# RWKV-7 chunk recurrence on Trainium2: the whole 64-block inverse ahead of the recurrence instead of a three-step solve inside it

## The chip, the cores and the metric

The kernel runs on one core of one Trainium2 chip. A core has a matrix engine (TensorE, PE in the profile, with PEld for its weight loads), a vector engine (VectorE, DVE), an activation engine (ScalarE, ACT), GpSimd (POOL), and a sync engine (SyncE, SP), whose queue here issues all DMA transfers. Each engine works off its own instructions in the order in which they were written, and waits where an operand is not there yet. The metric is device time in microseconds for one launch; lower is better.

## What the reference computes

One step of a decoder trunk of two layers, for 256 tokens of a prompt and 8 single tokens with saved states. In each layer a normalised input is projected; half of the columns go through RetNet retention (8 heads), half through RWKV-7 time mixing (16 heads of 64, worked on as 8 pairs); then come an output projection and a SwiGLU feed-forward network. The part that the change touches is the RWKV-7 scan over the prompt:

```
def step(s, inp):
    r_t, w_t, k_t, v_t, kk_t, a_t = inp
    sa = jnp.einsum('bhvk,bhk->bhv', s, -kk_t)
    s = (s * w_t[:, :, None, :] + sa[..., None] * (kk_t * a_t)[:, :, None, :]
         + v_t[..., None] * k_t[:, :, None, :])
    return s, jnp.einsum('bhvk,bhk->bhv', s, r_t)
```

Each step's `sa` depends on all earlier steps. Done in chunks of 64 tokens, that dependence inside a chunk is a unit lower triangular system (1 + L) Z = r, with L a 64x64 matrix for each head and chunk, and between chunks the state S is handed on.

## The kernel before

**The stream.** All weights (two layers, 6624 blocks of 128x128) are one stream. `Stream.load` fetches 8 blocks at a time (512 KB) into three `w_raw` buffers, on the sync queue; `Stream.make` splits four blocks at a time into a high part `w_hi` (ScalarE, L96) and a low part `w_lo` (VectorE, L99), three buffers of each, two groups of four ahead of the matmuls. Each block then multiplies the activations with three matmuls, in `proj` (L285 to L287) or in `contract` (L306 to L308). 

**The mixer between the blocks.** Every mixer step is a Python generator. After each block, `tick` lets those generators go on whose time has come; a generator's `yield n` means that n blocks are written before its next instructions. So the order of every engine's instructions is fixed when the program is written, and the yields are the only distance between an operand's producer and its reader on another engine. `need` and `take` tick without writing a block: if a slot of a pool is not free (`CAP`), all that is due is written out with no stream block between.

**A pair of RWKV heads.** `g_pair` prepares a pair: the triangular matrices `LA` and `KA` of its four chunks, and three transposed operands `TM` (three of eight slots that are shared with the tiles of the residual `h`). It may begin its later part only when the pair two before it has ended. `g_solve` (GpSimd) inverts the 16x16 diagonal blocks. `g_levels` merges pairs of them into inverses of 32x32 blocks, for four chunks at once: with the mask product m of L (L541, L526, GpSimd), Pm = m X (`pw<-X,Lm`, then a ScalarE copy, L549), and XT = XT - Pm XT (L552, L553). `X` and its transpose `XT` are then block diagonal with blocks of 32.

`g_seq` is the recurrence over the four chunks of a pair. For each chunk it writes: the product with `KA` and with the state S into `py` (L569, L571); from it `rT`, in two parts by VectorE and ScalarE (L574, L575); then the solve in three steps, `Z1` = X r (L587, copied by ScalarE at L590), `r1` = r - m1 Z1 (L594, subtracted by VectorE at L597) and Z = X r1 (L601, copied at L604); then the new state S (L607, L613) and the output (L617, L619). `m1` is the mask product for the second level, 32 to 64. Levels of one pair and the recurrence of another may overlap, but levels follow levels and recurrences follow recurrences (`spawn` with a kind).

**The layer.** `layer` writes the input projections of 8 pairs and 8 retention heads in the order of `ORDER`, then the output projection in three passes over 16 output blocks (`W_OUT`), during whose first pass `load_h` fetches the eight `h` tiles (each needs a `TM` slot), then the feed-forward network. Decode work for the single tokens (`g_rwkv_decode`: loads `dS`, products `dT`, reductions `dec_sa` and `dec_o`; `g_ret_state`: `rS`, `qkb`, `ryd`) runs beside it.

Of the kernel before, what the change touches and what calls it, by code (L numbers as in the profile page):

```python
# [11 lines left out]
F32 = mybir.dt.float32  # L12
F32R = mybir.dt.float32r
AF = mybir.ActivationFunctionType
ALU = mybir.AluOpType
# [4 lines left out]
P = 128  # L20
# [10 lines left out]
NC = SEQ // CW  # L31
# [13 lines left out]
TA, RR, LV, UB, U2 = 4, 2, 2, 6, 4  # L45
# [22 lines left out]
def bc(ap, axis, n):  # L68
    u = ap.unsqueeze(axis)
    s = list(u.shape)  # L70
    s[axis] = n
    return u.to_broadcast(s)
# [43 lines left out]


class Kern:
    """The main flow emits the weight stream: each 128x128 block is split into two float32r parts and multiplies the
    split activations in three passes. Every mixer step is a generator that yields the number of stream blocks to let  # L120
    pass before its next instructions, so that they reach the in-order engines when their operands are there."""

    def __init__(self, ctx, tc, a, o):
        self.tc, self.nc, self.a, self.o, self.ctx = tc, tc.nc, a, o, ctx
# [406 lines left out]
    def g_levels(self, t_solve, sv, LA):  # L531
        nc, rp = self.nc, self.rp
        yield from self.wait(t_solve)
        Xc = sv["X"]
        X = rp.tile([P, NC, P], F32, name="X", tag="lv", bufs=LV)
        XT = rp.tile([P, NC, P], F32, name="XT", tag="XT", bufs=2)

        def mm(lhsT, rhs):
            return lambda out, c: nc.tensor.matmul(out, lhsT=lhsT[:, c], rhs=rhs[:, c], start=True, stop=True)

        m = self.masked(LA, 0, "lv", LV)  # L541
        for q, t in enumerate((X, XT)):
            eng = nc.gpsimd if q else nc.vector
            eng.tensor_tensor(out=t.rearrange("p c (b k) -> p c b k", k=SB), in0=bc(Xc[:, q], 2, P // SB),
                              in1=bc(self.m_b8, 1, NC), op=ALU.mult)
        yield 8
        ps = yield from self.g_four(mm(m, X))
        Pm = rp.tile([P, NC, P], F32, name="Pm", tag="lv", bufs=LV)
        nc.scalar.activation(out=Pm, in_=ps, func=AF.Copy)  # L549
        self.pput()  # L550
        yield 5
        ps = yield from self.g_four(mm(Pm, XT))  # L552
        nc.vector.tensor_tensor(out=XT, in0=XT, in1=ps, op=ALU.subtract)  # L553
        self.pput()
        yield 4
        sv["XT"] = XT

    def g_seq(self, l, p, sv, AR, cf, LA, KA, TM, bv, Y):
        nc, rp, un = self.nc, self.rp, self.un
        XT = sv["XT"]  # L560
        m1 = self.masked(LA, 1, "m1", 1)
        o = rp.tile([P, 2, P], F32, name="o", tag="o", bufs=2)
        S = None
        lo, hi = slice(0, 64), slice(64, 128)
        for c in range(NC):
# [7 lines left out]
            rT = self.rT[:, c % 2]  # L573
# [8 lines left out]
                nc.scalar.activation(out=sc, in_=S, func=AF.Copy, scale=ct)  # L582
            pS = yield from self.pget()
            nc.tensor.matmul(pS[:, 0:P], lhsT=kT, rhs=vT, start=True, stop=False)
            yield 3
            pz = yield from self.pget()
            nc.tensor.matmul(pz[:, 0:P], lhsT=XT[:, c], rhs=rT, start=True, stop=True)  # L587
            yield 1
            Z1 = un.tile([P, P], F32, name="Z1", tag="u", bufs=UB)
            nc.scalar.activation(out=Z1, in_=pz[:, 0:P], func=AF.Copy)  # L590
            self.pput()
            yield 3
            pl = yield from self.pget()
            nc.tensor.matmul(pl[:, 0:P], lhsT=m1[:, c], rhs=Z1, start=True, stop=True)  # L594
            yield 1
            r1 = un.tile([P, P], F32, name="r1", tag="u", bufs=UB)
            nc.vector.tensor_tensor(out=r1, in0=rT, in1=pl[:, 0:P], op=ALU.subtract)  # L597
            self.pput()
            yield 3
            pz = yield from self.pget()  # L600
            nc.tensor.matmul(pz[:, 0:P], lhsT=XT[:, c], rhs=r1, start=True, stop=True)  # L601
            yield 1
            Z = un.tile([P, P], F32, name="Z", tag="Z", bufs=2)
            nc.scalar.activation(out=Z, in_=pz[:, 0:P], func=AF.Copy)  # L604
            self.pput()
            yield 3
            nc.tensor.matmul(pS[:, 0:P], lhsT=bT, rhs=Z, start=False, stop=True)  # L607
            yield 1
            Sn = un.tile([P, P], F32, name="S", tag="S", bufs=2)
# [2 lines left out]
            else:  # L612
# [6 lines left out]
            nc.vector.tensor_tensor(out=o[64 * (c % 2):64 * (c % 2) + 64, c // 2], in0=po[hi, 0:P], in1=oc[hi],  # L619
                                    op=ALU.add)  # L620
            self.pput()
            yield 2
        for hh in range(2):
            s = slice(64 * hh, 64 * hh + 64)
            nc.sync.dma_start(out=self.o["srp"][l, 2 * p + hh], in_=S[s, s])
# [808 lines left out]
```

## Time and profile before

| | us |
|---|---|
| three runs: median | 2919.91 |
| lowest, highest | 2918.66, 2921.32 |
| the profiled execution: its span, first to last instruction | 2925.0 |
| PE busy | 2799.1 (96%) |
| DVE busy | 2009.9 (69%) |
| ACT busy | 1416.1 (48%) |
| POOL busy | 806.9 (28%) |

The profile gives the span of its own execution and no other time of it. Busy time is the time in which at least one instruction of an engine is drawn; matmuls are pipelined, so their drawn ends overlap the next one's start. Every float32 matmul of the mixer is recorded as two, so that 64 calls (16 pairs x 4 chunks over two layers) are 128 records; a stream matmul is one record. An idle time in a row is that of the engine directly before the instruction, with the instruction that ended it.

### The profile page before, as it was taken

The page shows a single profiled execution, that of the slowest core. Times are in us where ns is not written, and L with a number is a line of the kernel's source. Part 1 is how long each engine was busy: PE and PEld are TensorE (multiplying, and loading weights), DVE is VectorE, ACT ScalarE, POOL GpSimd, SP SyncE. Part 2 cuts the span into 40 slices and gives each one's busy share as a digit, 9 for nine tenths or more (in the row PEclk, how much of TensorE's full clock was granted, in tenths as well). Part 3 has the DMA queues.
Part 4 walks back from the last instruction along what each step waited for, and adds up shares of the span by engine and source line. Part 5 has one row for each costly group of instructions (what it writes and reads, how often), then busy time and mean ns, then how long its engine had stood idle before and what let it go on. Part 6 is the DMA issues. An engine that isn't in the chain of part 4 may idle for free. (4 is left out here: it accounts for less than half of the span.)

```text
span 2925.0 us, 59208 instructions
## 1 busy us (share of the span) xinstructions
PE 2799.1 (96%) x22298; PEld 2755.2 (94%) x22298; DVE 2009.9 (69%) x3964; ACT 1416.1 (48%) x2823; POOL 806.9 (28%) x1316
## 2 busy tenths in 40 slices
PE   7998999999999999999999999999999999999998
PEld 7998999899999999999998888888999999999998
DVE  6677777887856656556766777778877565565665
ACT  5544455445444444444545445544544444444444
POOL 4545555434400000000234556554243000000002
PEclk9999999999999999999999999999999999999999
DMA  4454555565655555555654445556656555555554
GB/s 161 142 155 148 157 153 173 189 221 191 203 182 179 180 179 180 180 180 181 211 158 137 150 146 156 160 163 212 203 193 195 181 180 181 180 181 179 181 180 148
DMA packets 230832, 512.50 MB, mean 175 GB/s; under 512 B 57488, under 2 KB 105872, under 8 KB 230544
## 3 DMA queue, kind: packets, MB, share of 16 engines
q1 hardware_dynamic: 230544, 508.70, 54.6%
q8 instruction: 175, 2.87, 0.4%
q14 instruction: 113, 0.93, 0.1%
HBM read 485.24 MB, written 23.38 MB: 174 GB/s over the span
## 5 line engine op out<-in xcount | busy, mean ns | idle before, releaser
L99 DVE TENSOR_TENSOR w_lo<-w_raw,w_hi 128x512 fp32r<-128x512 f32 x1652 | 1240.4, 753 | 849.3 <-ACT w_hi L96 835.8
L96 ACT ACTIVATE w_hi<-w_raw 128x512 fp32r<-128x512 f32 x1656 | 1042.8, 631 | 1131.5 <-PE st L286 631.1
L285 PE MATMUL st<-blk,w_hi 128*128 128x264 f32 (+1 forms) x4704 | 1438.6, 306 | 11.9 <-ACT w_hi L96 7.4
L287 PE MATMUL st<-blk,w_lo 128*128 128x264 f32 (+1 forms) x4704 | 1353.0, 288 | 15.5 <-DVE w_lo L99 14.7
L286 PE MATMUL st<-blk,w_hi 128*128 128x264 f32 (+1 forms) x4704 | 1351.4, 287 | 1.0 <-DVE blk L1094 1.0
L287 PEld LDWEIGHTS st<-blk,w_lo 128*128 128x128 f32 x4704 | 895.0, 190 | 22.8 <-DVE w_lo L99 21.3
L285 PEld LDWEIGHTS st<-blk,w_hi 128*128 128x128 f32 x4704 | 896.2, 191 | 17.1 <-ACT w_hi L96 11.0
L286 PEld LDWEIGHTS st<-blk,w_hi 128*128 128x128 f32 x4704 | 898.0, 191 | 3.9 <-DVE blk L1094 2.0
L306 PE MATMUL st<-blk,w_hi 128*128 128x264 f32 x1920 | 551.0, 287 | 5.8 <-DVE h L1244 4.5
L307 PE MATMUL st<-blk,w_hi 128*128 128x264 f32 x1920 | 548.6, 286 | 0.0
L308 PE MATMUL st<-blk,w_lo 128*128 128x264 f32 x1920 | 546.7, 285 | 0.0
L1035 POOL TENSOR_TENSOR acc<-acc,sq 128x264 f32<-128x264 f32 x73 | 62.7, 860 | 1374.7 <-ACT sq L1032 1374.3
L306 PEld LDWEIGHTS st<-blk,w_hi 128*128 128x128 f32 x1920 | 361.0, 188 | 8.8 <-issue 4.0
L308 PEld LDWEIGHTS st<-blk,w_lo 128*128 128x128 f32 x1920 | 362.5, 189 | 0.1
L307 PEld LDWEIGHTS st<-blk,w_hi 128*128 128x128 f32 x1920 | 361.4, 188 | 0.1
L684 POOL TENSOR_TENSOR sv_t<-sv_m,sv_x 32x15 f32<-32x15 f32 (+7 forms) x240 | 90.0, 375 | 27.1 <-DMA sv_m<-scr_l 13.7
L1244 DVE TENSOR_TENSOR h<-h,st 128x264 f32<-128x264 f32 x224 | 94.1, 420 | 2.9 <-PE st L308 2.8
L686 POOL TENSOR_TENSOR sv_x<-sv_x,sv_t 32x15 f32<-32x15 f32 (+7 forms) x240 | 85.2, 355 | 18.8
L575 ACT ACTIVATE c_rT<-pw 64x64 f32<-64x64 f32 x64 | 13.8, 215 | 113.3 <-DVE c_rT L574 113.1
L323 ACT ACTIVATE mix_d<-mix_p,c_vec 128x256 f32<-128x256 f32 x54 | 27.5, 508 | 71.8 <-DVE mix_p L319 44.6
L899 POOL TENSOR_TENSOR qkb<-rS,qkb 128x512 f32<-128x512 f32 x32 | 44.5, 1391 | 58.9 <-DVE rS L896 58.9
L816 POOL TENSOR_TENSOR uS<-uS,dec_v 128x512 f32<-128x512 f32 x16 | 23.7, 1480 | 113.0 <-DMA uS<-in_s_rwkv 113.0
(251 smaller groups left out, 2636.5 us busy)
## 6 DMA issues: line engine op xcount, KB each, us to landing
w_raw<-in_ws SPq DMA_DIRECT2D x828, 512.0 KB
qkb<-scr_qk SPq DMA_DIRECT2D x64, 256.0 KB
rS<-in_s_ret SPq DMA_DIRECT2D x32, 256.0 KB
out_sts<-rS SPq DMA_DIRECT2D x32, 256.0 KB
h<-in_x SPq DMA_DIRECT2D x16, 264.0 KB
dS<-in_s_rwkv SPq DMA_DIRECT2D x16, 256.0 KB
uS<-in_s_rwkv SPq DMA_DIRECT2D x16, 256.0 KB
out_srs<-uS SPq DMA_DIRECT2D x16, 256.0 KB
```

Source lines behind the costliest of these rows:

```text
L96: nc.scalar.activation(out=h, in_=w, func=AF.Copy)
L99: eng.tensor_tensor(out=l, in0=w, in1=h.bitcast(F32), op=ALU.subtract)
L285: nc.tensor.matmul(ps, lhsT=hi, rhs=self.x[k][:, 0, 0:n], start=k == 0, stop=False)
L286: nc.tensor.matmul(ps, lhsT=hi, rhs=self.x[k][:, 1, 0:n], start=False, stop=False)
L287: nc.tensor.matmul(ps, lhsT=lo, rhs=self.x[k][:, 0, 0:n], start=False, stop=k == KB - 1)
L306: nc.tensor.matmul(ps, lhsT=hi, rhs=t[:, 0, 0:T], start=k == 0, stop=False)
L307: nc.tensor.matmul(ps, lhsT=hi, rhs=t[:, 1, 0:T], start=False, stop=False)
L308: nc.tensor.matmul(ps, lhsT=lo, rhs=t[:, 0, 0:T], start=False, stop=k == n - 1)
L684: nc.gpsimd.tensor_tensor(out=t, in0=bc(M[:, j, j + 1:SB], 2, j + 1), in1=bc(X0[:, j, 0:j + 1], 1, m), op=ALU.mult)
L686: nc.gpsimd.tensor_tensor(out=X0[:, j + 1:SB, 0:j + 1], in0=X0[:, j + 1:SB, 0:j + 1], in1=t, op=ALU.subtract)
L1035: nc.gpsimd.tensor_tensor(out=self.acc, in0=self.acc, in1=sq, op=ALU.add)
L1244: self.nc.vector.tensor_tensor(out=h, in0=h, in1=ps, op=ALU.add)
```

## The change

The loop over levels in `g_levels` now runs twice. The first pass is as before and ends with a transpose on VectorE, which works on blocks of 32x32: since `XT` is block diagonal in 32x32 blocks at that point, this gives the new `X`. The second pass uses the mask product `m1`, now made in the first pass, and leaves in `XT` the transposed inverse of the whole 64x64 block. `g_seq` then needs one matmul, Z = X r. The yields around it become 5, 1, 5 in place of 3, 1, 3, 1, 3, 1, 3, and the last one of a chunk 4 in place of 2. A comment of the class is replaced by blank lines. Code below the solve stands 8 lines further up than before. Its core:

```
@@ g_levels
-        ps = yield from self.g_four(mm(m, X))
-        Pm = rp.tile([P, NC, P], F32, name="Pm", tag="lv", bufs=LV)
-        nc.scalar.activation(out=Pm, in_=ps, func=AF.Copy)
-        self.pput()
-        yield 5
-        ps = yield from self.g_four(mm(Pm, XT))
-        nc.vector.tensor_tensor(out=XT, in0=XT, in1=ps, op=ALU.subtract)
-        self.pput()
+        for lev in range(2):
+            ps = yield from self.g_four(mm(m, X))
+            Pm = rp.tile([P, NC, P], F32, name="Pm", tag="lv", bufs=LV)
+            nc.scalar.activation(out=Pm, in_=ps, func=AF.Copy)
+            self.pput()
+            if lev == 0:
+                m = self.masked(LA, 1, "m1", 1)
+            yield 5
+            ps = yield from self.g_four(mm(Pm, XT))
+            nc.vector.tensor_tensor(out=XT, in0=XT, in1=ps, op=ALU.subtract)
+            self.pput()
+            if lev == 0:
+                X = rp.tile([P, NC, P], F32, name="X", tag="lv", bufs=LV)
+                nc.vector.transpose(X.rearrange("p c q -> p (c q)"), XT.rearrange("p c q -> p (c q)"))
+                yield 7
         yield 4
@@ g_seq
-        m1 = self.masked(LA, 1, "m1", 1)
...
             nc.tensor.matmul(pS[:, 0:P], lhsT=kT, rhs=vT, start=True, stop=False)
-            yield 3
+            yield 5
             pz = yield from self.pget()
             nc.tensor.matmul(pz[:, 0:P], lhsT=XT[:, c], rhs=rT, start=True, stop=True)
-            yield 1
-            Z1 = un.tile([P, P], F32, name="Z1", tag="u", bufs=UB)
-            nc.scalar.activation(out=Z1, in_=pz[:, 0:P], func=AF.Copy)
-            self.pput()
-            yield 3
-            pl = yield from self.pget()
-            nc.tensor.matmul(pl[:, 0:P], lhsT=m1[:, c], rhs=Z1, start=True, stop=True)
-            yield 1
-            r1 = un.tile([P, P], F32, name="r1", tag="u", bufs=UB)
-            nc.vector.tensor_tensor(out=r1, in0=rT, in1=pl[:, 0:P], op=ALU.subtract)
-            self.pput()
-            yield 3
-            pz = yield from self.pget()
-            nc.tensor.matmul(pz[:, 0:P], lhsT=XT[:, c], rhs=r1, start=True, stop=True)
             yield 1
             Z = un.tile([P, P], F32, name="Z", tag="Z", bufs=2)
             nc.scalar.activation(out=Z, in_=pz[:, 0:P], func=AF.Copy)
             self.pput()
-            yield 3
+            yield 5
...
-            yield 2
+            yield 4
```

How the order of instructions changes is shown at three places. The first is ScalarE in the recurrence of the first pair, one chunk, from its `rT` to its `Z`. Before:

```order
L575 ACTIVATE c_rT<-pw 64x64
L577 ACTIVATE oc<-pw 64x128
L582 ACTIVATE Sc<-S,cf 128x128
L96 ACTIVATE w_hi<-w_raw 128x512
L590 ACTIVATE Z_1926<-pw 128x128
L96 ACTIVATE w_hi<-w_raw 128x512 x2
L604 ACTIVATE Z<-pw 128x128
```

With the change:

```order
L581 ACTIVATE c_rT<-pw 64x64
L583 ACTIVATE oc<-pw 64x128
L588 ACTIVATE Sc<-S,cf 128x128
L96 ACTIVATE w_hi<-w_raw 128x512
L596 ACTIVATE Z<-pw 128x128
```

The copy `Z1` (L590, named Z_1926) and two splits of weights between it and `Z` are gone from the chunk.

The second place is VectorE at the levels of the first pair, with the stream's `w_lo` around it. Before:

```order
L553 TENSOR_TENSOR XT<-XT,pw 128x512
L99 TENSOR_TENSOR w_lo<-w_raw,w_hi 128x512
L319 TENSOR_TENSOR mix_p<-st,c_R 128x272
L574 TENSOR_SCALAR c_rT<-pw 64x64
L99 TENSOR_TENSOR w_lo<-w_raw,w_hi 128x512
```

With the change:

```order
L556 TENSOR_TENSOR XT<-XT,pw 128x512
L560 STREAM_TRANSPOSE X<-XT 128x512
L99 TENSOR_TENSOR w_lo<-w_raw,w_hi 128x512
L319 TENSOR_TENSOR mix_p<-st,c_R 128x272
L99 TENSOR_TENSOR w_lo<-w_raw,w_hi 128x512
```

The transpose follows directly on the subtraction, and the first `c_rT` of the recurrence is no longer here: the recurrence begins 24 blocks later, after a second subtraction into `XT`.

The third place is early in the output projection of the first layer, block 968 of 3312. The last stream matmul before and the first one behind are shown with what TensorE now has between them (TM, KA, AR, LA and XT are operands of pair 7's recurrence, `on` belongs to a retention head):

```order
L308 MATMUL st<-blk,w_lo 128x264
L575 MATMUL pw<-TM_6749,KA 128x128
L577 MATMUL pw<-S,AR 128x128
L590 MATMUL pw<-TM_6749,TM_6748 128x128
L593 MATMUL pw<-c_rT,XT 128x128
L599 MATMUL pw<-Z,TM_6747 128x128
L356 MATMUL pw<-c_ident,on 128x128 x2
L609 MATMUL pw<-Z,LA 128x128
L306 MATMUL st<-blk,w_hi 128x264
```

And VectorE between two `w_lo` at the same place, with the change:

```order
L611 TENSOR_TENSOR o<-pw,oc 64x128
L1236 TENSOR_TENSOR h<-h,st 128x264
L760 TENSOR_TENSOR dT<-dS,dec_wr 128x512
L762 TENSOR_REDUCE dec_o<-dT 128x8
L580 TENSOR_SCALAR c_rT<-pw 64x64
L1236 TENSOR_TENSOR h<-h,st 128x264
L710 TENSOR_SCALAR on<-ryt,bmv,brs 128x128 x2
L762 TENSOR_REDUCE dec_sa<-dT 128x8
L888 SCALAR_TENSOR_TENSOR rS<-rS,qkb_8113 128x512
L605 SCALAR_TENSOR_TENSOR S<-pw,cf,Sc 128x128
...
L99 TENSOR_TENSOR w_lo<-w_raw,w_hi 128x512
```

Left out are `dT`, o, `ry` and `dec_o`, one each. Before, the same position of both engines holds stream work with one or two mixer instructions between groups:

```order
L99 TENSOR_TENSOR w_lo<-w_raw,w_hi 128x512
L1244 TENSOR_TENSOR h<-h,st 128x264
L718 TENSOR_SCALAR on<-dec_o,bmv,brs 128x64
L650 SCALAR_TENSOR_TENSOR y<-y,c_vec,pw 128x256
L99 TENSOR_TENSOR w_lo<-w_raw,w_hi 128x512
```

What moved: the last chunk of pair 7, which before stood among the input projections up to block 928, now stands at block 968 in one piece, with what else was due. The second layer has the same place.

## Rows read from the trace of the kernel before

**Rows 1.** The page's first part: busy time (share of the span) x instructions.

```profile
PE 2799.1 (96%) x22298; PEld 2755.2 (94%) x22298; DVE 2009.9 (69%) x3964; ACT 1416.1 (48%) x2823; POOL 806.9 (28%) x1316
```

**Rows 2.** Stretches: length, busy PE, PEld, DVE, ACT, POOL (instructions), clock, DMA share, GB/s.

```profile
73.00:585.00 512.00, 473.42 (x3706) 459.82 (x3704) 381.18 (x875) 250.29 (x597) 271.50 (x504) 0.98 0.52 160
585.00:690.00 105.00, 102.30 (x826) 100.78 (x825) 85.73 (x167) 55.92 (x109) 38.98 (x56) 1.00 0.64 208
1530.00:2050.00 520.00, 478.18 (x3707) 461.33 (x3707) 394.62 (x909) 254.94 (x605) 279.71 (x504) 0.98 0.52 160
```

**Rows 3.** Waits of PE by line: total us, times, longest us.

```profile
PE pw L601 <- DVE r L597: 22.1, 20, 2.4
PE pw L587 <- ACT c_rT L575: 19.0, 17, 3.0
...
PE pw L571 <- DVE S L613: 5.0, 5, 3.0
...
PE pw L594 <- ACT Z L590: 2.0, 5, 0.9
PE pw L569 <- DVE S L613: 1.8, 2, 1.5
```

**Rows 4.** Timeline of PE around 331 us: start, length, instruction, [idle before, what ended it].

```profile
331.25 0.46 PE L601 MATMUL pw<-r,XT 128*128 128x128 f32 x2 [2.43 <-DVE r L597]
...
331.92 0.28 PE L285 MATMUL st<-blk,w_hi 128*128 128x264 f32 x1
332.04 0.29 PE L286 MATMUL st<-blk,w_hi 128*128 128x264 f32 x1
...
333.01 0.42 PE L286 MATMUL st<-blk,w_hi 128*128 128x264 f32 x1
333.23 0.42 PE L287 MATMUL st<-blk,w_lo 128*128 128x264 f32 x1
```

**Rows 5.** Stretches as in rows 2: first and last of six at half clock.

```profile
332.50:335.80 3.30, 3.30 (x17) 3.30 (x16) 2.07 (x4) 1.64 (x5) 2.79 (x3) 0.50 0.58 124
...
1970.90:1974.20 3.30, 3.30 (x17) 3.30 (x16) 3.30 (x5) 0.72 (x2) 3.30 (x3) 0.50 0.65 183
```

**Rows 6.** Groups of PE by shape: xcount | busy us, mean ns | idle before, what ended it.

```profile
L601 PE MATMUL pw<-r,XT 128*128 128x128 f32 x128 | 27.2, 294 | 22.3 <-DVE r L597 22.1
...
L539 PE MATMUL pw<-X,Lm 128*128 128x128 f32 x128 | 25.7, 283 | 5.6 <-DVE bst L706 4.0 <-DVE X L544 1.6
```

**Rows 7.** Groups of DVE by shape, columns as in rows 6.

```profile
L99 DVE TENSOR_TENSOR w_lo<-w_raw,w_hi 128x512 fp32r<-128x512 f32 x1652 | 1240.4, 753 | 849.3 <-ACT w_hi L96 835.8 <-PE pw L356 2.2 <-PE st L287 1.7
L1244 DVE TENSOR_TENSOR h<-h,st 128x264 f32<-128x264 f32 x224 | 94.1, 420 | 2.9 <-PE st L308 2.8
...
L896 DVE SCALAR_TENSOR_TENSOR rS<-rS,qkb 128x512 f32<-128x512 f32 x32 | 22.3, 698 | 6.5 <-POOL qkb L894 6.5
...
L597 DVE TENSOR_TENSOR r<-c_rT,pw 128x128 f32<-128x128 f32 x64 | 17.7, 277 | 1.2 <-PE pw L594 0.9
...
L544 DVE TENSOR_TENSOR X<-sv_c,c_m_b 128x512 f32<-128x512 f32 x16 | 14.4, 903 | 3.7 <-DMA sv_c<-scr_x 3.7
L574 DVE TENSOR_SCALAR c_rT<-pw 64x64 f32<-64x64 f32 x64 | 13.6, 212 | 3.1 <-PE pw L571 2.0
...
L768 DVE TENSOR_TENSOR dT<-dS,dec_wr 128x512 f32<-128x512 f32 x16 | 12.6, 787 | 0.1
L718 DVE TENSOR_SCALAR on<-ryt,bmv,brs 128x128 f32<-128x128 f32 x32 | 12.6, 435 | 1.5 <-POOL brs L714 1.5
...
L770 DVE TENSOR_REDUCE dec_sa<-dT 128x8 f32<-128x512 f32 x16 | 10.9, 679 | 6.2 <-POOL dT L768 6.2
L553 DVE TENSOR_TENSOR XT<-XT,pw 128x512 f32<-128x512 f32 x16 | 10.8, 677 | 0.0
```

**Rows 8.** Groups of ACT by shape, columns as in rows 6.

```profile
L590 ACT ACTIVATE Z<-pw 128x128 f32<-128x128 f32 x64 | 17.7, 277 | 7.0 <-PE pw L587 5.9
...
L549 ACT ACTIVATE Pm<-pw 128x512 f32<-128x512 f32 x16 | 9.5, 593 | 4.1 <-PE pw L539 3.9
```

## The prediction, made before the changed kernel was run

> **What bounds the kernel now.** I read the busy shares first: TensorE is busy 96% of the span [rows 1], so TensorE is the queue that sets the end, and everything is a question of when it waits or runs slowly. Its work is one stream of weight blocks, three matmuls each, with the mixer's small matmuls between them; the engine takes them strictly in the order written. In the stretches by stage [rows 2] the two mixer stages (73 to 585 us and 1530 to 2050 us) are where TensorE has holes: 473.42 busy of 512 us and 478.18 of 520 us. VectorE is busy three quarters of that time. The next stage, the output projection, has almost no hole (102.30 of 105 us), but there VectorE is busy 85.73 of 105 us. So what the change can win lies in the holes of the mixer stages, and what it can lose lies in a place where VectorE has little room.
>
> The list of waits names the holes [rows 3]. The largest is the second solve matmul (L601), which waits for VectorE's `r1`: 22.1 us in 20 waits. The second is the first solve matmul (L587), which waits for `rT`: 19.0 us in 17 waits, the longest 3.0 us. Behind them stand L571 and L569, which wait for the new state S, and L594. The timeline of one of them [rows 4] shows how a wait is to be read. A stream matmul starts 0.12 us after the one before it (331.92, 332.04) although each is drawn 0.28 us long. So a block is worth 3 x 0.12 = 0.36 us, and an idle time as listed hides about 0.16 us more. The same timeline shows, after the wait of 2.43 us at 331.25, starts that are 0.22 us apart (333.01, 333.23): TensorE has fallen to its lower level, 1.2 GHz.
>
> **What the change removes.** Sixteen pairs times four chunks lose the two middle steps, L594 and L601, with the ScalarE copy `Z1` and the VectorE subtraction `r1`.
> - Waits: 22.1 + 2.0 = 24.1 us in 25 waits [rows 3]; with 25 x 0.16 = 4 us hidden by the drawn ends, and some 3 us for waits too short to be listed (103 of the 128 calls show none), I take **-31 us** (24 to 34).
> - L587 stays but is now written five yields after its operands' producers instead of three. Two blocks are at least 0.73 us of cover. Taken off 17 waits of 1.1 us on average that is at most 12.4 us; the longest keeps over 2 us. With the hidden parts I take **-13 us** (7 to 17).
> - L571 and L569 wait for S 5.0 + 1.8 us in 7 waits [rows 3]. The last yield of a chunk grows from two to four, so 7 x 0.73 = 5 us at most: **-4 us** (0 to 7).
> - The lower clock: eleven such stretches lie between the start and the end, and six of them follow directly on a wait of L601, L587 or L569 (the first and the last are [rows 5], granted clock 0.50). 17 matmul records fit into 3.3 us there; at 0.12 us spacing it would be 27. So each costs about 10 x 0.12, or 1.3 us. Up to 6 x 1.3 = 8 us can go; since the rarer waits are partly the long ones that stay, **-4 us** (0 to 8).
>
> The sum of what goes is 52 us (31 to 66).
>
> **What it adds.** The second pass of the level loop costs, for each of sixteen pairs, eight 128x128 matmuls, a copy `Pm`, a subtraction into `XT` and a 32x32-block transpose of `XT` into `X`. The mask product on GpSimd is only written earlier.
> - TensorE's calls: 128 go (2 x 64) and 128 come (16 x 8). They cost the same, 294 and 283 ns a record [rows 6], and both kinds stand alone between stream blocks. **0 us.**
> - ScalarE: 64 copies of 277 ns go, 17.7 us; 16 of 593 ns come, 9.5 us [rows 8]. It has room. 0 us.
> - VectorE: 64 subtractions of 277 ns go, 17.7 us; 16 of 677 ns come, 10.8 us [rows 7], and 16 transposes. No transpose is in this trace. The nearest rows with 128x512 elements between SBUF tiles run from 679 to 903 ns (L770, L544), so I take 0.7 us, 11 us in all, with 0.3 us (c_rT, 212 ns, is about the smallest row) and 1.6 us as ends. VectorE's busy time so grows by about 4 us net. The order shows the transpose directly behind the subtraction, a lump of 1.4 us on the queue from which `w_lo` and `c_rT` also come. The engine's lateness grows a little for all who wait for it: **+3 us** (0 to 10).
> - The Trainium skill (VectorE: DVE Perf Modes, The three transpose paths) gives 311 ns for a 128x128 bf16 transpose in 32x32 blocks; an estimate from it is four of those, 1.24 us. By it VectorE would have 9 us more to do, and the sum would be at the upper half of the term above. No run here shows it yet.
> - The first matmul of the second pass needs subtraction and transpose. It stands ten blocks behind the last matmul of the first pass, 3.6 us at least, against 1.4 us of work plus VectorE's lateness. The first pass's own entry idles 5.6 us in 16 groups [rows 6] with eight blocks of cover: **+3 us** (0 to 8).
>
> **What it moves.** A pair's levels now take 53 yields instead of 29, its recurrence 72 instead of 80, so each pair ends later, and the last pair of a layer by more than 50 blocks. The order shows the consequence in the output projection. Pair 7 holds three of the eight `TM` slots until its recurrence is written out; the load of the sixth `h` tile, at block 968 of the layer, asks for a slot, finds none, and the program writes out all of the last chunk (and whatever else is due) without one stream block between. It happens in both layers. In the kernel before pair 7 was through by block 928. There TensorE gets the naked chain:
> - On VectorE an addition to h (420 ns), `dT` (787), a reduction (about 679) and `c_rT` (212) stand ahead [rows 7]: 2.1 us. Then the copy of `rT`, a matmul, the copy `Z`, a matmul, each about 0.28 us: some 1.2 us. TensorE idles about 3.4 us.
> - Behind `c_rT`, VectorE has up to the next `w_lo`: an addition to h 0.42, two `on` 0.87, `dec_sa` 0.68, `rS` 0.70, `dT` 0.79, `dec_o` about 0.68 [rows 7], and S, o and `ry`, estimated at 0.35 each from L597 and L1244: 5.2 us. Then `w_lo` itself, 0.75 us. So `w_lo` comes at 2.1 + 6.0 = 8.1 us, later if `rS` or `dec_sa` wait for GpSimd, as they do now for 6.5 and 6.2 us in 11 places [rows 7]. TensorE, started again at 3.4 us with two groups of four blocks ready (2.9 us), runs dry at 6.3 us: another 2 us of idle.
> - A lower-clock stretch behind it, 1.3 us by the row above.
>
> That is 7 us a layer, **+14 us** (4, if only the chain of copies is seen, to 26, if both waits for GpSimd fall in and the sync queue's next weight load is late too: it stands behind the stores of `rS` and S and behind the h load).
>
> TensorE's clock is the point on which a rule speaks against the change. Here the clock fell right behind single idle times of 1.5 to 3 us. The Trainium skill (TensorE: Matmul & The Clock Gate, Why this matters for your kernels) wants no idle gaps between matmul bursts since the clock falls back to the lower level. The trace agrees; by the rule alone the two new gaps each buy one slow stretch, which is in the 14 us.
>
> The sum of what comes is 20 us (4 to 44).
>
> **How the numbers follow.** The page's own execution has a span of 2925.0 us, 5.1 us (0.17%) over the median of the three runs, 2919.9; no other time of it is given, so I make the sum as a difference and take it off the median. -52 + 20 = -32: **2888 us**. All best ends together give 2919.9 - 62 = 2858, all worst 2933. The terms are nearly independent.
>
> The cases, with about 0.2% (5.8 us) as what a measurement of this kernel can tell from no change:
> - **Forecast**, 0.45: as summed, 2888 (2876 to 2899).
> - **Full relief**, 0.22: the extra yields and the missing step leave VectorE time to catch up, the gap in the projection costs 4 us a layer or less, and the transposes disappear: 2919.9 - 60 + 8 = 2868. For it: VectorE is idle a quarter of the mixer stages.
> - **The lateness moves on**, 0.22: VectorE's queue is what is late, not the step. Waits of L601 then show up at S, `c_rT`, `w_lo` and the new first matmul; only L594, the short waits and half of L601 go. 2919.9 - 15 - 10 + 14 = 2909 (2903 to 2917). For it: VectorE ends most of the listed waits and gets no less work. Against it: the long waits are single ones, and `w_lo` is made two groups ahead.
> - **No shorter path**, 0.05: the step was never on the path; what TensorE loses at L601 is caught up at the next `w_hi`. 2919. Against it: TensorE starts the next block at once after each wait [rows 4].
> - **Slower**, 0.06: the gap in the output projection. VectorE waits there for GpSimd, GpSimd for decode loads issued in the same lump, and the sync queue holds the next weight load behind two stores that wait for VectorE. It decides from (52 + 6) / 2 = 29 us a layer on; at 35 us a layer the time is 2919.9 - 52 + 6 + 70 = 2944.
>
> Faster by more than 0.2%: 0.45 + 0.22 + three quarters of 0.22 = 0.83; within 0.2%: 0.05 + the rest of 0.22 = 0.11; slower: 0.06. The range 2865 to 2912 leaves out about a tenth at each end.
>
> **What would show it.** In the profile after, L601's and L594's waits are gone; the matmul on `rT` should wait 10 us or less in all; the new matmul `pw<-X,Lm` of the second pass a few us; the transpose about 0.7 us. Early in the output projection each layer should show one idle time of about 3 us before `pw<-c_rT,XT` and one before a stream matmul that waits for `w_lo`. Fewer stretches at half clock. I am wrong if the waits for VectorE add up to as much as before under other names, if the gap is over 15 us a layer, or if the transpose takes over 2 us.

## The result, and the profile after

| | median, us | lowest, highest |
|---|---|---|
| before (4 runs) | 2920.61 | 2918.66, 2922.64 |
| after (4 runs) | 2951.72 | 2948.51, 2954.38 |

The change makes the kernel slower: ratio 1.0106, 95% interval 1.0092 to 1.0120, 31 us where 32 us less were predicted. The profiled execution after has a span of 2952.6 us, 27.6 us more than that of before.

The page's first part of after answers to [rows 1]: busy time (share of the span) x instructions.

```profile
PE 2812.9 (95%) x22298; PEld 2770.3 (94%) x22298; DVE 2022.6 (69%) x3932; ACT 1406.5 (48%) x2775; POOL 804.5 (27%) x1316
```

TensorE has the same 22298 instructions, VectorE 32 fewer. So no work was added that would account for 28 us; it is time in which TensorE waits or is slow. Where it lies can be read by stream blocks, which both kernels have in the same order. The table takes, from the traces, the time between the matmuls of two blocks of the stream; a layer's mixer is blocks 192 to 912, then come the last input projections and the first pass of the output projection up to block 1008. The second layer's blocks are 3312 higher. Differences are to before, profile against profile; the rows below the first two belong to the experiments. "1.2 GHz" is the time at that level between the start and the end of the program, "rT wait" the idle time before the first solve matmul (L587 before, L593 after).

| kernel | 192-912 | 912-1008 | 3504-4224 | 4224-4320 | 1.2 GHz | rT wait |
|---|---|---|---|---|---|---|
| before, us | 437.7 | 48.3 | 443.5 | 48.4 | 37.5 | 19.5 |
| after | -10.7 | +19.9 | -7.0 | +25.2 | 78.5 | 33.7 |
| e2_hold | -2.8 | +6.3 | +0.3 | +5.7 | 54.6 | |
| e13_noblock | -11.7 | +22.3 | -8.6 | +28.4 | 68.3 | |
| e7_y3 | -3.3 | +3.2 | +1.2 | +1.5 | 58.0 | 33.3 |
| e8_y4 | +10.7 | +9.4 | -4.3 | +12.5 | 88.8 | 34.0 |
| e4_rTact | -18.7 | +16.6 | -13.4 | +23.8 | 75.1 | 4.0 |
| e5_before_rTact | -8.4 | +0.5 | -0.3 | 0.0 | 47.8 | 3.7 |
| e9_y3_rTact | -13.7 | +1.7 | -15.7 | +1.1 | 41.0 | 4.0 |
| e10_y4_rTact | -15.0 | +5.7 | -13.8 | +11.8 | 51.2 | |
| e11_y3_rTact_c2 | -9.6 | -1.0 | -10.4 | +0.7 | 51.2 | 3.2 |
| e12_y3_tr2 | -0.1 | +3.5 | +6.5 | +1.5 | 58.0 | |
| e14_y3_rTvec | -0.1 | +2.6 | +3.5 | +0.6 | 68.3 | 34.4 |

The profiled execution of e4_rTact lies 10 us above that kernel's median, that of e14_y3_rTvec 6 us above and that of e10_y4_rTact 5 us below, and their rows are to be read with that in mind.

All other blocks of after together give 0.2 us. So the two mixers together gain 17.7 us, and the 96 blocks behind each of them lose 45.1 us together. A part of both is only the work that changed sides. The stretches of after, answering to [rows 2] (length, busy PE, PEld, DVE, ACT, POOL with instructions, clock, DMA share, GB/s):

```profile
116.70:543.70 427.00, 397.59 (x3139) 388.30 (x3138) 322.37 (x702) 211.09 (x493) 232.46 (x428) 0.98 0.51 159
543.70:611.90 68.20, 54.41 (x394) 51.73 (x392) 55.63 (x151) 25.33 (x64) 27.32 (x32) 0.92 0.63 202
1567.40:2004.00 436.60, 405.97 (x3151) 393.74 (x3149) 325.90 (x711) 213.81 (x499) 238.37 (x437) 0.98 0.49 155
2004.00:2077.60 73.60, 55.58 (x394) 52.02 (x393) 57.67 (x157) 25.27 (x64) 27.62 (x35) 0.92 0.63 199
```

The stretch behind the mixer holds 394 matmul records, 49 more than the same blocks of before (345), most of them of pair 7's last chunks. At 0.12 us a record, the spacing of stream matmuls in [rows 4], they are an estimated 5.9 us a layer. What is left is a loss of 14 us in the first layer and 19 in the second, and a gain in the mixers of 18 - 12 = 6 us.

The list of waits of after (PE's, total us, times, longest) answers to [rows 3]:

```profile
PE pw L593 <- ACT c_rT L581: 27.4, 16, 3.8
PE st L287 <- DVE w_lo L99: 22.9, 32, 2.0
PE pw L539 <- DVE X L544: 9.5, 6, 2.4
...
PE st L306 <- POOL blk L820: 6.1, 2, 3.2
PE pw L577 <- DVE S L605: 3.7, 3, 1.6
PE pw L593 <- ACT oc L583: 3.3, 3, 1.6
...
```

L601 and L594 are gone with their 24.1 us. But L593, written two blocks later than L587 was, waits longer than L587 did (19.0 us), and the wait before L539 has grown from 5.6 us [rows 6] to 9.5. All of L593's idle times together are 33.7 us. Of these, 10.9 us lie behind the mixers, where 8 of the 64 chunks are now written; the 56 chunks inside them have 22.7 us. ScalarE is named for `c_rT`, but it is not the cause. What that line itself waits for says so (line L581 of after: its engine's idle time, us and times):

```profile
its engine sat idle before it (us, times) until:
  DVE c_rT L580: 159.4, 61
```

The two parts of `rT` go into one tile, and ScalarE's stands behind VectorE's in 61 of 64 chunks. One such place, in the first layer's mixer. Timeline of PE in after (start, length, instruction, idle before):

```profile
510.79 0.39 PE L577 MATMUL pw<-S,AR 128*128 128x128 f32 x2
...
511.38 0.39 PE L590 MATMUL pw<-TM,TM 128*128 128x128 f32 x2
...
517.19 0.80 PE L593 MATMUL pw<-c_rT,XT 128*128 128x128 f32 x2 [3.60 <-ACT c_rT L581]
```

and VectorE's timeline there:

```profile
509.21 2.70 DVE L99 TENSOR_TENSOR w_lo<-w_raw,w_hi 128x512 fp32r<-128x512 f32 x2
511.94 0.29 DVE L611 TENSOR_TENSOR o<-pw,oc 64x128 f32<-64x128 f32 x1
512.25 1.15 DVE L710 TENSOR_SCALAR on<-ryt,bmv,brs 128x128 f32<-128x128 f32 x2
513.32 0.68 DVE L544 TENSOR_TENSOR X<-sv_c,c_m_b 128x512 f32<-128x512 f32 x1
513.92 0.68 DVE L99 TENSOR_TENSOR w_lo<-w_raw,w_hi 128x512 fp32r<-128x512 f32 x1
514.52 1.06 DVE L739 TENSOR_TENSOR dec_sq<-dec_v 128x64 f32<-128x64 f32 x1
515.61 0.22 DVE L741 TENSOR_REDUCE dec_n<-dec_sq 128x1 f32<-128x64 f32 x1
...
516.67 0.22 DVE L580 TENSOR_SCALAR c_rT<-pw 64x64 f32<-64x64 f32 x1
```

The product that `rT` is made from is done at about 511.2 us. Its 0.2 us of VectorE come at 516.67, because eleven instructions are written ahead of it, behind a `w_lo` under way, and VectorE has no hole between them. Two more blocks of distance, 0.73 us, are little against 5.5 us, and the stream's own `w_lo` stands in the same queue.

Behind the mixer, the waits of PE from 543.7 to 615 us in after:

```profile
PE pw L593 <- ACT c_rT L581: 3.3, 1, 3.3
PE st L306 <- POOL blk L820: 2.9, 1, 2.9
PE st L306 <- DVE bst L698: 2.2, 1, 2.2
PE pw L593 <- ACT oc L583: 1.6, 1, 1.6
PE pw L577 <- DVE S L605: 1.6, 1, 1.6
PE st L308 <- DVE w_lo L99: 1.4, 1, 1.4
...
```

The first and the fifth are the lump's own chain, at 582 and 578 us. Another, the wait for `blk` (L820), lies at 611 us, at the start of the second pass of the projection (block 1008). That pass multiplies with pairs 0 to 3, whose block needs its decode columns (`put` at L820), and `g_rwkv_decode` writes those only when all eight pairs have their output (`while not all(self.outs)`). A late pair 7 therefore blocks the program twice: at block 968 for a `TM` slot, and at block 1008 for the decode part. In the order of after, nineteen yields at block 968 and three at block 1008 are written without a stream block in the first layer, twenty-one and six in the second; before has none at these places.

The clock adds to it. Three stretches of after behind the mixers, columns as in rows 2:

```profile
581.00:587.80 6.80, 5.50 (x24) 5.21 (x25) 3.87 (x9) 1.68 (x5) 3.33 (x4) 0.52 0.15 45
611.00:617.80 6.80, 6.58 (x26) 6.09 (x27) 3.24 (x6) 1.03 (x2) 5.50 (x19) 0.53 0.53 161
2045.00:2051.80 6.80, 5.62 (x24) 5.12 (x25) 4.21 (x10) 2.25 (x7) 2.92 (x5) 0.50 0.27 82
```

Each lies at one of the waits told above or at its like in the second layer, and lasts twice as long as those of [rows 5]. In all, after runs 78.5 us at 1.2 GHz where before ran 37.5. By the prediction's price (1.3 us lost in 3.3) the 41 us more cost an estimated 16 us, half of the whole loss. The rows behind the mixers bear that price out. TensorE's idle times there add up to 13.8 us in the first layer and 18.0 in the second, against 3.6 in each of before, so 10.2 and 14.4 us of the 14 and 19 are waits. That leaves 8.7 us in both layers, and 22.9 us at 1.2 GHz lie there (none in before), by the price 9.0.

### The profile page after: what moved, and what is told of

The parts are those of the page before. It is cut to its first block, busy times and chain, and to the rows that moved or that the text cites. A ratio compares the mean times of both kernels' runs of the same rounds, so it can differ in the third digit from the quotient of the medians.

```text
span 2952.6 us, 59100 instructions
## 1 busy us (share of the span) xinstructions
PE 2812.9 (95%) x22298; PEld 2770.3 (94%) x22298; DVE 2022.6 (69%) x3932; ACT 1406.5 (48%) x2775; POOL 804.5 (27%) x1316
## 4 chain that ended last, share of the span: by engine, by line
PE 68%; DVE 7%; POOL 3%; DMA 2%; issue 2%; ACT 1%; SPq 1%; DVEq 0%; POOLq 0%; ACTq 0%
PE st L287 14%; PE st L285 14%; PE st L286 13%; PE st L307 8%; PE st L306 8%; PE st L308 8%; DVE w_lo L99 2%; PE pw L539 1%; DMA dS<-in_s_rwkv 1%; POOL sv_t L676 1%; POOL sv_x L678 1%; ACT w_hi L96 1%; DMA w_raw<-in_ws 1%; PE pw L360 1%; PE pw L419 1%
## 5 line engine op out<-in xcount | busy, mean ns | idle before, releaser
L285 PE MATMUL st<-blk,w_hi 128*128 128x264 f32 (+1 forms) x4704 | 1434.3, 305 | 11.4 <-ACT w_hi L96 7.3
L287 PE MATMUL st<-blk,w_lo 128*128 128x264 f32 (+1 forms) x4704 | 1354.1, 288 | 24.2 <-DVE w_lo L99 22.9
L285 PEld LDWEIGHTS st<-blk,w_hi 128*128 128x128 f32 x4704 | 895.8, 190 | 16.6 <-ACT w_hi L96 11.0
L306 PE MATMUL st<-blk,w_hi 128*128 128x264 f32 x1920 | 557.9, 291 | 12.2 <-POOL blk L820 6.1
L307 PE MATMUL st<-blk,w_hi 128*128 128x264 f32 x1920 | 554.3, 289 | 0.3 <-POOL blk L821 0.3
L581 ACT ACTIVATE c_rT<-pw 64x64 f32<-64x64 f32 x64 | 13.8, 215 | 159.4 <-DVE c_rT L580 159.4
L324 POOL TENSOR_SCALAR mix_d<-mix_p,c_vec 128x8 f32<-128x8 f32 x54 | 23.2, 429 | 164.0 <-DVE mix_p L319 163.8
L539 PE MATMUL pw<-X,Lm 128*128 128x128 f32 x256 | 52.7, 289 | 9.5 <-DVE X L544 9.5
```

The costliest lines, as they stand in the source:

```text
L285: nc.tensor.matmul(ps, lhsT=hi, rhs=self.x[k][:, 0, 0:n], start=k == 0, stop=False)
L287: nc.tensor.matmul(ps, lhsT=lo, rhs=self.x[k][:, 0, 0:n], start=False, stop=k == KB - 1)
L306: nc.tensor.matmul(ps, lhsT=hi, rhs=t[:, 0, 0:T], start=k == 0, stop=False)
L307: nc.tensor.matmul(ps, lhsT=hi, rhs=t[:, 1, 0:T], start=False, stop=False)
```

## The experiments

Theory: two things went wrong, each of its own. In the mixers, `rT` waits in VectorE's order, and more cover hardly helps, so the missing steps give little. Behind them, the recurrence ends 40 blocks later and meets the projection's gates. Rivals: the lump at block 968 alone is the loss; the transposes' work on VectorE is; ScalarE is, because it stands idle behind VectorE.

**The lump alone (e2_hold).** The kernel before, with pair 7 keeping its slots 58 blocks longer, so that the sixth `h` tile finds none; nothing else is late.

```diff
-        self.rel("TM", "TM", "TM")
         self.spawn(self.g_out(l, p, o, bv, Y), 1, "out")
+        self.spawn(self.g_hold(58 if p == NP - 1 else 0))
+    def g_hold(self, n):
+        yield n
+        self.rel("TM", "TM", "TM")
```

> The kernel before, with one thing of the change alone: pair 7 of each layer keeps its three TM slots for 58 more blocks after its recurrence (which ends where it did), so that the load of the sixth h tile finds no slot at block 968 and some 20 yields' worth of mixer work is written without a stream block between, as in the changed kernel, but without the recurrence's last chunk in it. Theory 'slot' (the lump that the missing slot makes is what costs, by VectorE's queue and the lower clock behind it): 5 to 20 us a layer, 2930 to 2960 us. Rival 'late tail' (the cost comes from the recurrence and the decode work that now end later, not from the lump): no more than 4 us off the kernel before, 2917 to 2925 us.

Measured: 2932.66 us against 2922.57, ratio 1.0036 (1.0023 to 1.0049), 10 us. In the table each layer loses about 6 us behind its mixer, an estimated 1 us of it for ten more records. So a lump at block 968 costs something of the size that the prediction gave its own, about a third of the loss. It is not the lump of after, though: no chunk is in it, and in the first layer its longest wait, 5.4 us, is for decode work (`o`).

**Ending earlier (e7_y3, e8_y4).** The changed kernel with the two yields of 5 around the solve as 3, and as 4. Pair 7's last chunk is then through at block 924 or 950 of the first layer, against 968 in after.

```diff
-            yield 5
+            yield 3
             pz = yield from self.pget()
...
-            yield 5
+            yield 3
             nc.tensor.matmul(pS[:, 0:P], lhsT=bT, rhs=Z, start=False, stop=True)
```

> The changed kernel with the two long yields of a chunk's solve set back from 5 to 3. A chunk takes 14 blocks, pair 7 ends at block 924 as in the kernel before (928), no slot is missing, and decode ends as early as before. Slot and late tail both expect the loss in the output projection to go, about 20 us a layer and more with the clock: 2905 to 2925 us, the upper half if the shorter cover gives back the 13 us that I had put on it. Rival (the loss comes with the second level's work wherever it stands): 2940 us or more.

> The changed kernel with the same two yields at 4. Pair 7 ends at block 950, 22 blocks later than before, but no slot is missing and nothing is written in a lump. Slot expects the whole loss in the output projection to go: 2905 to 2918 us. Late tail expects about half of it to stay, since the decode work still ends some 16 blocks late: 2925 to 2940 us.

Measured: 2927.69 us, ratio 1.0016 (1.0005 to 1.0026), with 3; 2952.53, ratio 1.0100 (1.0085 to 1.0115), with 4. The first lies 3 us above the range that both theories gave it, the second 12 us above the slower of its two. Ending at block 924 takes back 24 us of the 31. The stretch behind the mixer in e7_y3:

```profile
553.80:605.30 51.50, 45.35 (x347) 42.60 (x346) 46.63 (x112) 20.86 (x49) 22.54 (x39) 1.00 0.68 224
```

347 records, granted clock 1.00; in its order no yield is written without a stream block here, so both gates are open when the stream arrives. In e8_y4 nothing blocks at block 968, yet 9.4 and 12.5 us are lost behind the mixers, of which an estimated 2 us each are moved work (363 and 364 records). In the second layer three yields are written without a stream block at the second gate, block 4320; in the first there is no gate, so there lateness costs without a lump. Its first mixer loses 10.7 us too, which no theory had foreseen: TensorE idles 5.3 us more in it than before, and has 20.5 us more at 1.2 GHz.

The distance from `rT` to its reader, its cover, is one block shorter in e8_y4 than in after, two in e7_y3, and the waits of the whole program, 34.0 and 33.3 us as against 33.7, look as if cover did nothing. But after's hold the 10.9 us behind the mixers. Inside the mixers a chunk waits 0.53 us with a yield of 3 (32.6 us, 62 chunks), 0.55 with 4 (32.4 us, 59) and 0.41 with 5 (22.7 us, 56; 0.42 in e13_noblock). So one block more does nothing and two take about a quarter off, each read from one profiled execution.

**The lump removed, the lateness left (e13_noblock).** The changed kernel, in which the load of an `h` tile no longer stops the program: it is a generator that waits for its slot beside the stream.

```diff
-                    self.load_h(l, k // 2 + 2)
+                    hl[k // 2 + 2] = self.spawn(self.g_load_h(l, k // 2 + 2), 0)
...
+    def g_load_h(self, l, j):
+        yield from self.acq("TM")
...
+    def g_add(self, k, ps, load):
+        yield 0
+        yield from self.wait(load)
+        self.adder(k, ps)()
```

> The changed kernel with the loads of the h tiles written by a generator that waits for its slot without holding up the stream; the additions into a late tile wait with it. No lump is left at block 968. But the recurrence still ends at block 982, and the second pass of the output projection, from block 1008, needs the decode part of pairs 0 to 3, which waits for all eight pairs: in the program's order 22 and 27 yields' worth of work are now written there without a stream block (3 and 6 in the changed kernel). Slot: the loss of the changed kernel mostly goes, 2912 to 2942 us. Late tail: the lump only moves to the next gate, 2944 to 2962 us.

Measured: 2952.87 us, ratio 1.0110 (1.0095 to 1.0126), the time of after. Its waits of PE from 542 to 615 us:

```profile
PE st L306 <- POOL blk L820: 6.1, 1, 6.1
PE st L306 <- DVE h L1250: 5.8, 4, 2.0
...
```

The gate at block 968 is gone, the last chunk ends at block 982, and the gate at block 1008 takes 6.1 us in place of 2.9. The additions into late `h` tiles (L1250) cost 5.8 us as well. So the slot was only the first of several things that a late pair 7 holds up, and removing it hands the wait to the others.

**rT off VectorE (e4_rTact, e5_before_rTact).** Both parts of `rT` are made by ScalarE, in the changed kernel and in the kernel before.

```diff
-            nc.vector.tensor_scalar(out=rT[lo, lo], in0=py[lo, lo], scalar1=-1.0, scalar2=None, op0=ALU.mult)
+            nc.scalar.activation(out=rT[lo, lo], in_=py[lo, lo], func=AF.Copy, scale=-1.0)
```

> The changed kernel with both parts of rT copied by ScalarE, so that nothing between the product py and the solve matmul passes through VectorE's queue. Theory 'VectorE's lateness is what the recurrence waits for': the 33.7 us that TensorE idles before the matmul on rT mostly go, 2915 to 2935 us, with the lump in the output projection still there but shorter by 2 to 3 us a layer. Rival (ScalarE is as late, or another operand is next): within 6 us of the changed kernel, 2946 to 2958 us.

> The kernel before with both parts of rT copied by ScalarE, as in the run of that kind on the changed kernel. VectorE's lateness: the 19 us that TensorE idles at the first solve matmul mostly go and the 22 us at r1, which VectorE still makes, stay: 2895 to 2910 us. Rival (what is taken off the wait for rT comes back at r1, whose VectorE queue is as late): 2914 to 2926 us.

Measured: 2927.48 us for the changed kernel, ratio 1.0016 (1.0006 to 1.0026); its rT wait falls from 33.7 to 4.0 us. (Its profiled execution lies 10 us above its median, so that its row in the table is good for that wait only.) The kernel before comes to 2913.78, ratio 0.9976 (0.9966 to 0.9986). The same edit gives 24 us there and 7 here. Why, the waits of e5_before_rTact show:

```profile
PE pw L601 <- DVE r L597: 31.0, 18, 3.7
...
PE pw L587 <- ACT c_rT L575: 3.7, 5, 1.9
```

L587's 19.0 us became 3.7, and L601's 22.1 became 31.0: of the 15.3 us taken off the first wait, 8.9 came back at the second. The chunk has a lateness of VectorE to sit out, and the second instruction of the chain on that engine takes over more than half of it when the first is cured.

**Both together (e9_y3_rTact, e10_y4_rTact).** The changed kernel with both parts on ScalarE and yields of 3, or of 4.

> The changed kernel with the two yields at 3 (no lump, recurrence ends at block 924) and both parts of rT on ScalarE. If the two losses are the late tail and VectorE's lateness at rT and they add, 2927.7 - 24 = 2904, range 2890 to 2912 us. If the changed solve is worth something beyond that, it is also below the kernel before with the same rT; if not, the two are equal or this one is slower. Rival (ScalarE, which with shorter cover is as late): 2918 to 2930 us.

> As the run with the yields at 3 and rT on ScalarE, with the yields at 4. Pair 7 ends at block 950. Late tail expects 10 to 20 us more than with 3, since the decode work ends 16 blocks later: 2910 to 2930 us. Slot alone, without a late tail, expects it equal or faster, 2888 to 2905 us, since the cover is longer.

Measured: **2901.17 us** with 3, ratio 0.9933 (0.9918 to 0.9947), faster than both kernels; 2919.90 with 4, ratio 0.9997 (0.9987 to 1.0007). Waits of PE in e9_y3_rTact:

```profile
PE st L287 <- DVE w_lo L99: 30.7, 38, 3.1
...
PE pw L577 <- DVE S L605: 4.8, 7, 1.1
...
PE pw L593 <- ACT c_rT L581: 2.8, 2, 2.3
```

The solve hardly waits now; `w_lo` has taken over (14.7 us before). In the table both mixers gain some 14 to 16 us and less than 2 us is lost behind each. The two cures add up: ending in time is worth some 25 us, and rT on ScalarE as much again. With both cured, the change itself is worth 2913.78 - 2901.17 = 12.6 us (the two ran on one chip, against the same runs of the kernel before). With 4, the time is 19 us longer, as the late tail had it (10 to 20), and the 96 blocks behind the second mixer still lose 11.8 us.

**Whose queue it is (e14_y3_rTvec), and the transpose's price (e12_y3_tr2).** The yields are 3 in both. In the first, VectorE makes both parts of `rT`, ScalarE none; in the second, the transpose is written twice.

```diff
-            nc.scalar.activation(out=rT[hi, hi], in_=py[lo, hi], func=AF.Copy, scale=-1.0)
+            nc.vector.tensor_scalar(out=rT[hi, hi], in0=py[lo, hi], scalar1=-1.0, scalar2=None, op0=ALU.mult)
```

```diff
                 nc.vector.transpose(X.rearrange("p c q -> p (c q)"), XT.rearrange("p c q -> p (c q)"))
+                nc.vector.transpose(X.rearrange("p c q -> p (c q)"), XT.rearrange("p c q -> p (c q)"))
```

> The changed kernel with yields of 3 around the solve, and both parts of rT made by VectorE (ScalarE makes none). Theory: the matmul on rT waits because rT stands in VectorE's queue behind other work; taking only ScalarE's part away leaves that, so the waits before L593 stay at 30 us or more (33.3 in the kernel with yields of 3) and the time near 2927 us (2922 to 2932). Rival: what costs is that ScalarE stands idle at the head of its own queue behind VectorE's part (129.9 us in 64 places) and makes w_hi late; then the time falls to about 2901 us, as when both parts are ScalarE's, and the waits before L593 to under 10 us.

> The changed kernel with yields of 3 around the solve, and the transpose written twice, the second into the same tile: 16 x 0.71 = 11.4 us more on VectorE, nothing else. It measures the transpose's own price. Theory (VectorE has holes here, and what hurts is a single instruction that stands behind others at the wrong moment): 2928 to 2932 us, 0 to 4 over the kernel without it. Rival (every microsecond on VectorE in the mixer stages is paid by TensorE): 2939 us, the full 11 over it.

Measured: 2930.99 us, ratio 1.0029 (1.0018 to 1.0041), and 2934.70, ratio 1.0039 (1.0024 to 1.0053), with 2922.68 for the kernel before. The wait of e14_y3_rTvec, and the two transposes of e12_y3_tr2 (groups: xcount | busy us, mean ns | idle before):

```profile
PE pw L593 <- DVE c_rT L581: 34.3, 24, 4.0
```

```profile
L560 DVE STREAM_TRANSPOSE X<-XT 128x512 f32<-128x512 f32 x16 | 11.4, 712 | 0.6
L561 DVE STREAM_TRANSPOSE X<-XT 128x512 f32<-128x512 f32 x16 | 11.4, 711 | 0.6
```

With ScalarE out of it the wait is the same, 34.3 us: it is VectorE's order, not ScalarE's idling. 11.4 us more on VectorE cost 2934.70 - 2927.69 = 7 us, some 5 us either way by the two intervals, between the two expectations of 0 to 4 and 11. So the transposes' work costs something, some 12 of the 31 us at most, but this run does not settle whether TensorE pays all of their time or less than half.

**Still earlier (e11_y3_rTact_c2).** The fastest version with the last yield of a chunk back from 4 to 2.

```diff
-            yield 4
+            yield 2
         for hh in range(2):
```

> The fastest version so far (yields of 3 around the solve, both rT parts on ScalarE: 2901 us) with the last yield of a chunk back from 4 to 2, as in the kernel before. The recurrence gets shorter by eight blocks a pair, so pair 7 ends still earlier, and the state S gets two blocks less of cover before the next chunk's L577. Theory (once pair 7 ends ahead of the output projection, nothing is gained by ending earlier, while S, now 4.8 us in 7 waits, has less cover): 2901 to 2906. Rival (work that ends earlier still relieves the projection): 2895 to 2899.

Measured: 2908.84 us, ratio 0.9953 (0.9937 to 0.9970), about 6 us slower than with 4 (by the ratios; the intervals just overlap). Its waits:

```profile
PE pw L577 <- DVE S L605: 9.4, 7, 2.3
...
PE pw L539 <- DVE X L560: 5.3, 4, 2.6
```

Those for S double from 4.8 us, and the second pass of the levels begins to wait for its transposed X. Both expected ranges lay below this time (2901 to 2906, 2895 to 2899). Ending earlier than block 924 brings nothing more.

## Why the prediction was wrong

The prediction summed a relief of 52 us and a price of 20. In the profile, moved work left out, the mixers gave 6 us of relief and the 96 blocks behind them took 33. Two steps failed: each listed wait was taken as a cost of its own instruction, and the one lump was taken as all that a later end does. Two of the three signs that it named for being wrong are there: waits for VectorE that add up to as much as before under other names, and, in the second layer, more than 15 us lost in the projection (19 net; 14 in the first).

- **Waits of L601 and L594, -31.** They are gone, but not the time. The idle before the solve matmuls went from 41.8 us (L601 and L587) to 33.7 (L593), that before `w_lo` from 14.7 to 22.9, before L539 from 5.6 to 9.5. With L594 and S (2.0 and 6.8 before, 0 and 4.3 after) the sums are 70.9 and 70.4 us. The equality is partly chance, since after's sum holds the 10.9 us of L593 that lie behind the mixers. The mixers alone show it cleaner, in e7_y3, which has no lump and the same 62 chunks there: TensorE's idle times before the matmuls of the solve and those with KA and S fall from 52.4 to 33.4 us, and all its others rise from 16.7 to 31.5, so 15 of the 19 us come back under other names. The time at 1.2 GHz rises there from 27.3 to 47.8 us. The step that failed is the subtraction of listed waits as if each were a cost of its own instruction. They were for the most part one lateness of VectorE, met at the next instruction of the chain or of the stream; e5_before_rTact shows it moving from L587 to L601 in the kernel before. This is the rival "the lateness moves on", which had 0.22.
- **L587 with more cover, -13.** Wrong in sign: +14 us (19.5 to 33.7), 3 of them in the mixers and 11 behind them. That cover helps was right, and its size was not far off: 0.41 us a chunk with 5 against 0.53 with 3 is an estimated 7 us over 62 chunks. What failed is the wait that it was taken off. At the old distance of 3 it is 33.3 us (e7_y3) and not 19.5, because the lateness that r1 had met is met here, and two blocks bridge little of 5.5 us of instructions written ahead on an engine without holes.
- **The wait for S, -4.** About right: 6.8 to 4.3 us before L577, and e11_y3_rTact_c2 shows that the longer last yield earns it.
- **The lower clock, -4.** Wrong in sign: an estimated +16 by the same price. There are 16 stretches between the start and the end instead of 11, and seven of the 16 last 6.8 us.
- **TensorE and ScalarE at no cost.** Right: 22298 instructions as before, 289 and 274 ns a record for the matmuls of the levels (the first is in the rows below), and ScalarE 10 us less busy than before.
- **The transpose, 0.7 us each.** 712 ns measured. The estimate of 1.24 us from the Trainium skill (VectorE: DVE Perf Modes, The three transpose paths) was too high; the trace decides. What 16 of them cost is not well known: about 7 us, give or take 5, if the first writing is worth what the second is in e12_y3_tr2. The term of 3 us (0 to 10) was for the net load, of which 4 us were expected; VectorE's busy time grew by 12.7 us (2009.9 to 2022.6), and no run shows where all of that comes from.
- **The second pass's entry, +3.** It hardly waited: all 9.5 us before L539 with X are for the first pass's X (L544). The groups of after:

```profile
L539 PE MATMUL pw<-X,Lm 128*128 128x128 f32 x256 | 52.7, 289 | 9.5 <-DVE X L544 9.5
...
L560 DVE STREAM_TRANSPOSE X<-XT 128x512 f32<-128x512 f32 x16 | 11.4, 712 | 0.6
...
L550 ACT ACTIVATE Pm<-pw 128x512 f32<-128x512 f32 x32 | 18.9, 589 | 7.3 <-PE pw L539 7.1
```

- **The lump in the projection, +14.** Its own price was about right, somewhat low: in the first layer its waits are 3.3 + 1.6 + 1.4 us (5.4 were expected) and its slow stretch 6.8 us (3.3 expected). What failed is that the place was taken for the whole consequence of a later end. The second gate (decode of all pairs ahead of the second pass) stood in the code and was not looked for, and late work in the projection costs without any gate (an estimated 7 us in the first layer of e8_y4). The slower rival had the right place and the right mechanism, but was asked to outweigh a relief of 52 us that wasn't there. With a relief of 6 us it decides from (6 + 6) / 2 = 6 us a layer on. Its chain, as the timeline of after has it in the lump, VectorE waiting for GpSimd and GpSimd for a decode load:

```profile
583.80 1.27 POOL L760 TENSOR_TENSOR dT<-dS,dec_v 128x512 f32<-128x512 f32 x1 [5.62 <-DMA dS<-in_s_rwkv]
...
585.11 0.69 DVE L762 TENSOR_REDUCE dec_sa<-dT 128x8 f32<-128x512 f32 x1 [2.62 <-POOL dT L760]
```

- **The rule on the clock** (the Trainium skill, TensorE: Matmul & The Clock Gate, Why this matters for your kernels), idle gaps between matmul bursts lower the clock: the trace agrees, 37.5 to 78.5 us at 1.2 GHz. The prediction let each gap buy one stretch of 3.3 us; the three shown last 6.8 us.

Open remain why the first mixer of e8_y4 waits more and runs longer at 1.2 GHz than that of e7_y3, and how the waits behind the mixers divide exactly between the two gates and the late work. No run here removes both gates and keeps the end at block 968; the nearest, the first layers of e8_y4 and e10_y4_rTact, have no gate and end at block 950.

## What to carry to other kernels

Before a listed wait is subtracted, look at what stands ahead of its producer on the producer's engine: if it is a full queue, a shorter chain mostly moves the wait to the next operand from there. Here moving the one small instruction to an engine with holes was worth more (some 25 us) than the algebra (12.6 us). When a change lets a stage end later, list every gate that the next stage has on that end, not the first one that the order shows. Distances can outweigh the change itself: here four yields fewer a chunk turn 31 us of loss into 5.

## What the runs showed of the hardware

VectorE's instructions do not have one length. For one form, `dT` on VectorE, after shows these (least, median and longest in ns):

```profile
L760 DVE TENSOR_TENSOR dT<-dS,dec_wr x16: 648/686/1764, 521.2 to 2051.8; 128x512 f32<-128x512 f32 x16
```

One of 1.73 us runs beside a GpSimd instruction of 1.28 us in the lump (586.97 and 586.88 us), as do the other three long ones. Two that took no longer than the rest also ran beside one for a part of their time. Whether GpSimd is the cause was not tried. Stretches at 1.2 GHz are not of one length either: 3.3 us behind the single waits of [rows 5], 6.8 us at the lumps of after, and 6.8 us also around the single wait of 3.60 us at 517 us, in the mixer.
